# Shift and scale of layer 0: sums over input channels moved from TensorE to GpSimd and VectorE

## The chip, the core and the metric

One core of a Trainium2 chip runs the kernel. Five engines work side by side, each through its own queue in order: PE (TensorE; PEld are its weight loads), DVE (VectorE), ACT (ScalarE), POOL (GpSimd) and SP (SyncE, which here only issues DMAs). They meet at semaphores. The metric is the time of one execution in microseconds (us), the median of several runs.

## The reference

Two layers of a decoder trunk on x of 1024 positions by 1024 channels. Each layer begins with a normalisation of the rows of x that is modulated by the vector c; the modulation is what this document is about:

```python
c_act = jax.nn.silu(c)
for l in range(DEPTH):
    mod = c_act @ w_ada[l] + b_ada[l]
    shift, scale, gate = jnp.split(mod, 3, axis=-1)
    h = rmsnorm(x, g_pre[l]) * (1.0 + scale[:, None, :]) + shift[:, None, :]
    p = h @ w_in[l]
    ...
    y = jnp.concatenate([y_conv, y_attn], axis=-1) @ w_out[l]
    x = x + gate[:, None, :] * rmsnorm(y, g_post[l])
```

`w_ada` has 1024 input channels and 3072 columns. Between `p` and `y` lie a gated convolution and a sparse attention, which the change does not touch.

## The kernel before

All work on 1024 positions is cut into tiles of 128 rows (128 partitions). Matrix products that need full precision split each f32 operand into a high and a low part and make three passes (lines 87 to 89: high·high, high·low, low·high); the splitting of a weight is `load_w` (line 107 on ACT makes the high part, line 108 on POOL subtracts it).

Layer 0 begins in `first`. It needs four things from memory, all issued by SP in the order of the table `LOADS`: the eight row tiles of x (four in `xs` early, four late), the weights of shift and scale (`wa`), and the first columns of `w_in` (`wr`). The weights of shift and scale are laid out by output channel: chunk k of eight holds, for the 128 channels k, the 256 columns of shift and scale and all 1024 input channels. The input channels are cut into eight groups of 128, one channel of a group on each partition, so a chunk comes as two tiles of 128 x 1024, `ws[0]` with groups 0 to 3 and `ws[1]` with groups 4 to 7, and `ws[j // 4][:, j % 4]` is the 128 x 256 piece of group j. `cact` (128 x 8) holds silu(c) in the same layout.

`mod_cols(k, ...)` turns chunk k into 128 values of shift and 128 of scale. Eight matmuls of 32 output rows (line 171) multiply the pieces with `cact` and sum over the partitions and over groups j and j + 4; DVE copies the result out of PSUM (line 173); two matmuls against `sel` (line 176) add the four quarters and put the 256 sums on partitions. DVE adds the bias (line 179, `modc`) and makes the factor of the normalised row (line 180, `moda`).

The loop of `first` runs over k. It calls `mod_cols` for chunk k + 1 ahead of the work on chunk k, loads and splits `wr` on even k, and for chunk k and the first four row tiles transposes x (line 297, PE), applies `moda` and `modc` (line 299, ACT, into `hf`), splits into high and low (lines 301 and 302, DVE, into `hT`), and multiplies with the split `w_in` columns into four PSUM sums `cp` (12 matmuls per chunk). Only when all eight chunks are done come the last four row tiles (`columns(4, 8)`) and their products, and then the rest of the layer. The rows are normalised by a square sum on ACT (line 287), two small POOL instructions (lines 265 and 268, `rx`) and a multiplication on DVE (line 928).

The `wa` tiles use the buffers that `hT` takes over afterwards. The order of instructions in each engine's queue is not written by hand: a scheduler fixes it when the program is built, from the order of the code and its own estimate of times.

Of the kernel before, what the change touches and what calls it, by code (L numbers as in the profile page):

```python
# [19 lines left out]
OP = mybir.AluOpType  # L20
# [3 lines left out]
P = 128  # L24
# [27 lines left out]
def hybrid_kernel(ctx: ExitStack, tc: tile.TileContext, x, cT, w_ada, w_mod, bcol, bgate, g_pre, w_in, w_cp,  # L52
# [3 lines left out]
    V, S, G, T = nc.vector, nc.scalar, nc.gpsimd, nc.tensor  # L56
# [19 lines left out]
    def mm_ps(name="mm"):  # L76
        return ps.tile([P, 512], F32, name=name, tag="mm", bufs=2)
# [65 lines left out]
    cact = cst.tile([P, 8], F32, name="cact")  # L143
    V.scalar_tensor_tensor(cact, cth, 1.0, ct, op0=OP.add, op1=OP.mult)
    V.tensor_scalar(cact, cact, 0.5, None, op0=OP.mult)
    pick = cst.tile([P, 8], F32, name="pick")
    V.memset(pick, 0.0)
    V.memset(pick[:, 5:6], 1.0)
    for q in range(4):
        V.memset(pick[32 * q:32 * q + 1, q:q + 1], 1.0)  # L150
        V.memset(pick[32 * q:32 * q + 1, 4:5], 1.0)
    pick4, sel, ones = pick[:, 0:4], pick[:, 4:5], pick[:, 5:6]
    x1d = dr.tile([L, D], F32, name="x1d")
    gd = dr.tile([depth, 1024], F32, name="gd")
    ad = dr.tile([4, P, 1024], F32, name="ad")
# [7 lines left out]
        MOD[l] = (bc, gp, cst.tile([P, 2, 8], F32, name="modc", tag="modc"),  # L163
                  cst.tile([P, 8], F32, name="moda", tag="moda"))

    def mod_cols(k, ws, row):

        o = mm_ps("mod")
        for j in range(8):
            q = j % 4  # L170
            T.matmul(o[32 * q:32 * q + 32, :256], cact[:, j:j + 1].to_broadcast([P, 32]), ws[j // 4][:, j % 4],
                     start=j < 4, stop=j >= 4)
        V.tensor_copy(row, o[:, :256])
        t = mm_ps("modt")
        for j in range(2):
            T.matmul(t[:, j:j + 1], row[:, 128 * j:128 * j + 128], sel, start=True, stop=True)
        bc, gp, mc, a = MOD[0]
        ks = slice(k, k + 1)
        V.tensor_tensor(mc[:, :, ks], t[:, 0:2].rearrange("p (c h) -> p c h", c=2), bc[:, :, ks], op=OP.add)
        V.scalar_tensor_tensor(a[:, ks], mc[:, 1, ks], 1.0, gp[:, ks], op0=OP.add, op1=OP.mult)  # L180
# [198 lines left out]
    def first(xs, wa, wr):  # L379
# [14 lines left out]
        def mod(k):  # L394
            if k < 8:
                mod_cols(k, wa[k], row[:, k % 4])
                if k % 2 == 0:
                    c.w.append(load_cw(0, k // 2, wr[:, 456 * k:456 * k + 912]))
# [734 lines left out]
```

## Time and profile before

| | |
|---|---|
| median of 3 runs | 1255.23 us (1254.13 to 1255.27) |
| the profiled execution | 1254.51 us |
| its span, first to last instruction | 1252.8 us |
| busy share of the span | PE 95%, PEld 78%, DVE 73%, ACT 55%, POOL 50% |
| instructions | 23059 |

The span is the stretch from the first to the last instruction of the program; the execution's own time is 1.7 us longer. All stretches below are counted from the span's start. The profile gives busy time by engine, by stretch and by group of instructions; the idle time of an engine is put down to what ended it. A group's line names the line of the kernel, engine, operation, what is written and read, and the shape.

### The profile page before, as it was taken

What the parts mean: (1) busy time and instruction counts of PE and PEld (TensorE: products, weight loads), DVE (VectorE), ACT (ScalarE), POOL (GpSimd) and SP (SyncE); (2) the same over time, 40 slices, a digit from 0 to 9 for tenths busy, and PEclk for the clock granted to TensorE, in tenths of its full rate; (3) what the DMA queues carried; (4) which work ended last, traced back from release to release, by engine and by line L of the source; (5) the groups of instructions that cost most, each with busy time, mean ns of one, the idle gap of its engine ahead of it and who ended that gap; (6) DMA issues with size and microseconds to landing.
All of it is one profiled execution on the core that took longest, in us unless ns stands there. A gap on an engine that the chain in (4) does not pass through costs nothing. (4 is left out here: it accounts for less than half of the span.)

```text
span 1252.8 us, 23059 instructions
## 1 busy us (share of the span) xinstructions
PE 1188.3 (95%) x7832; PEld 974.9 (78%) x7832; DVE 915.3 (73%) x2239; ACT 688.1 (55%) x1580; POOL 628.0 (50%) x1222
## 2 busy tenths in 40 slices
PE   6999999898998999999999999989979899999998
PEld 3888888557886777789988888866768677777998
DVE  3667899999777667757686579989985866677214
ACT  3645768667626556522355466877682465564221
POOL 3441146447536457855585202554673465588222
PEclk9999999899999999999999999989989899999999
DMA  9411266771010000137751123767111100012215
GB/s 360 144 51 34 52 206 209 243 250 52 11 43 21 9 9 26 52 108 267 241 202 53 44 51 107 233 209 211 55 32 28 34 10 5 5 54 74 74 35 185
DMA packets 90854, 128.10 MB, mean 102 GB/s; under 512 B 41320, under 2 KB 68464, under 8 KB 90736
## 3 DMA queue, kind: packets, MB, share of 16 engines
q1 hardware_dynamic: 90736, 126.63, 31.6%
q8 instruction: 62, 1.02, 0.3%
q14 instruction: 56, 0.46, 0.1%
HBM read 114.01 MB, written 12.59 MB: 101 GB/s over the span
## 5 line engine op out<-in xcount | busy, mean ns | idle before, releaser
L528 DVE TENSOR_SCALAR_CACHE_REDUCE jv<-pl,cand 128x768 int16<-128x768 uint16 (+1 forms) x186 | 187.8, 1009 | 17.7 <-DVE jv L528 6.6
L525 ACT ACTIVATE ja<-pl,cand 128x896 int8<-128x896 uint16 (+1 forms) x186 | 153.8, 827 | 40.6 <-POOL cand L535 34.8
L803 ACT ACTIVATE p<-p,mx 128x128 f32<-128x128 f32 (+7 forms) x128 | 98.8, 772 | 55.1 <-DVE mx L800 53.1
L805 POOL TENSOR_SCALAR p<-p,ri 128x128 f32<-128x128 f32 (+7 forms) x128 | 99.8, 784 | 43.8 <-DVE ri L804 43.5
L108 POOL TENSOR_TENSOR wul<-raw,wuh 128x342 fp32r<-128x342 f32 (+1 forms) x48 | 48.6, 1022 | 132.1 <-ACT wuh L107 116.9
L89 PE MATMUL o<-woh,yl 128*128 128x256 f32 x384 | 108.7, 283 | 2.1 <-POOL yl L861 2.1
L87 PE MATMUL o<-woh,yh 128*128 128x256 f32 x384 | 109.4, 286 | 0.5 <-DVE yrr L903 0.5
L88 PE MATMUL o<-wol,yh 128*128 128x256 f32 x384 | 108.5, 283 | 0.0
L87 PE MATMUL g<-hT,wgh 128*128 128x512 f32 x256 | 103.3, 404 | 2.6 <-ACT ya L688 2.2
L89 PE MATMUL g<-hT,wgl 128*128 128x512 f32 x256 | 102.3, 399 | 0.0
L88 PE MATMUL g<-hT,wgh 128*128 128x512 f32 x256 | 101.6, 397 | 0.0
L87 PE MATMUL u<-hT,wuh 128*128 128x512 f32 x256 | 100.8, 394 | 0.0
L88 PE MATMUL u<-hT,wuh 128*128 128x512 f32 x256 | 100.0, 391 | 0.0
L89 PE MATMUL u<-hT,wul 128*128 128x512 f32 x256 | 99.9, 390 | 0.0
L817 PE MATMUL pt<-ident,p 128*128 128x128 f32 x576 | 94.6, 278 | 2.4 <-ACT pt L822 1.7
L790 POOL TENSOR_TENSOR p<-tb,score 128x256 f32<-128x256 f32 x96 | 71.2, 749 | 48.2 <-PE pt L817 46.1
L843 PE MATMUL av<-pt,v 128*64 128x256 f32 (+1 forms) x640 | 93.3, 368 | 0.0
L461 DVE SCALAR_TENSOR_TENSOR score<-relu,widx,score 128x384 f32<-128x384 f32 (+2 forms) x84 | 79.2, 976 | 18.4 <-ACT relu L453 17.5
L817 PEld LDWEIGHTS pt<-ident,p 128*128 128x128 f32 x576 | 67.4, 140 | 25.5 <-issue 10.9
L822 ACT ACTIVATE pt<-pt 128x512 f32<-128x512 f32 (+2 forms) x96 | 50.2, 523 | 64.4 <-PE pt L817 63.8
L453 ACT ACTIVATE relu<-ixs 128x512 f32<-128x512 f32 (+2 forms) x140 | 66.4, 522 | 34.5 <-PE ixs L447 34.1
L447 PE MATMUL ixs<-ix 128*128 128x512 f32 (+2 forms) x320 | 76.3, 356 | 0.4 <-DVE ix L436 0.4
(302 smaller groups left out, 3463.6 us busy)
## 6 DMA issues: line engine op xcount, KB each, us to landing
wt<-in_wl_dram SPq DMA_DIRECT2D x64, 512.0 KB, 5.1
wa<-in_w_mod_dram SPq DMA_DIRECT2D x32, 512.0 KB, 5.2
raw<-in_w_in_dram SPq DMA_DIRECT2D x64, 171.0 KB, 2.5
wa<-in_w_ada_dram SPq DMA_DIRECT2D x16, 512.0 KB, 9.8
raw<-in_w_out_dram SPq DMA_DIRECT2D x32, 171.0 KB, 2.4
raw<-in_w_in_dram SPq DMA_DIRECT2D x32, 170.0 KB, 2.6
ad<-A SPq DMA_DIRECT2D x8, 512.0 KB, 3.3
at<-ad SPq DMA_DIRECT2D x16, 256.0 KB, 6.5
```

Of the source, the lines that this page charges most:

```text
L87: T.matmul(o, ah, bh, start=first, stop=False)
L88: T.matmul(o, ah, bl, start=False, stop=False)
L89: return T.matmul(o, al, bh, start=False, stop=last)
L447: mark = T.matmul(o[:, :c1 - c0], s_[:, 128 * i:128 * i + 128], ix[:, kk, c0:c1], start=kk == 0, stop=kk == 1)
L461: V.scalar_tensor_tensor(acc, r[:, :w], wc, acc, op0=OP.mult, op1=OP.add)
L525: S.activation(ja[:, :wid(j)], src, AF.Sign, scale=-1.0, bias=col(cand, c), accum_out=col(ct_, c))
L528: V.tensor_scalar(jv[:, :wid(j)], src, col(cand, c), None, op0=OP.is_lt, op1=OP.add, accum_out=col(ct_, c))
L790: G.tensor_tensor(nb, tb, sc[:, OFF[i] + n0:OFF[i] + w], op=OP.add)
L803: mark[0] = S.activation(p[:, :w], p[:, :w], AF.Exp, scale=-1.0, bias=m[:, 2:3], accum_out=ri[:, 0:1])
L805: mark[1] = G.tensor_scalar(p[:, :w], p[:, :w], ri[:, 1:2], 1.0, op0=OP.mult, op1=OP.mult)
L817: T.transpose(t[:, 128 * j:128 * j + 128], p[:, 128 * (j0 + j):128 * (j0 + j) + 128], ident)
L843: T.matmul(o[64 * e:64 * e + 64, t0:256], lh, pts[e][j // 4][:, j % 4, t0:256], start=j == 0, stop=j == 2 * c + 1)
```

## The change

Only `mod_cols` changes. The sum over the eight groups of a partition's channels is taken out of the matmuls. Groups 0 to 2 are multiplied in place by `cact` on POOL and added into group 0 (three multiplications and two additions of 128 x 256). Group 3 is multiplied on DVE into a sum `acc`, groups 4 to 7 are multiplied and added on DVE, and at the end the POOL part is added. Two matmuls against a column of ones then sum over the partitions, where `sel` picked four rows before. PSUM holds no `mod` sum any more, and line 173's copy out of PSUM is gone. Lines behind the function move by 3 (299 becomes 302, 301 becomes 304, 302 becomes 305).

```diff
-    pick4, sel, ones = pick[:, 0:4], pick[:, 4:5], pick[:, 5:6]
+    pick4, ones = pick[:, 0:4], pick[:, 5:6]
...
-    def mod_cols(k, ws, row):
-
-        o = mm_ps("mod")
-        for j in range(8):
-            q = j % 4
-            T.matmul(o[32 * q:32 * q + 32, :256], cact[:, j:j + 1].to_broadcast([P, 32]), ws[j // 4][:, j % 4],
-                     start=j < 4, stop=j >= 4)
-        V.tensor_copy(row, o[:, :256])
+    def mod_cols(k, ws, acc):
+
+
+        for j in range(3):
+            G.tensor_scalar(ws[0][:, j], ws[0][:, j], cact[:, j:j + 1], 1.0, op0=OP.mult, op1=OP.mult)
+            if j:
+                G.tensor_tensor(ws[0][:, 0], ws[0][:, j], ws[0][:, 0], op=OP.add)
+        V.tensor_scalar(acc, ws[0][:, 3], cact[:, 3:4], None, op0=OP.mult)
+        for j in range(4, 8):
+            V.scalar_tensor_tensor(acc, ws[1][:, j - 4], cact[:, j:j + 1], acc, op0=OP.mult, op1=OP.add)
+        V.tensor_tensor(acc, acc, ws[0][:, 0], op=OP.add)
         t = mm_ps("modt")
-        for j in range(2):
-            T.matmul(t[:, j:j + 1], row[:, 128 * j:128 * j + 128], sel, start=True, stop=True)
+        for h in range(2):
+            T.matmul(t[:, h:h + 1], acc[:, 128 * h:128 * h + 128], ones, start=True, stop=True)
```

The scheduler places the new instructions among the old ones. On POOL, before, from the normalisation of the fourth row tile to that of the fifth (`wc1l` to `wc3` are low parts of `w_in`, three instructions each):

```order
L265 TENSOR_SCALAR rxv_278<-ssx_278 128x1
L268 TENSOR_TENSOR rx_280<-rxv_278,mhalf_71 128x1
L108 TENSOR_TENSOR wc1l_312<-wr_129,wc1h_311 128x304 x3
L108 TENSOR_TENSOR wc2l_402<-wr_129,wc2h_401 128x304 x3
L108 TENSOR_TENSOR wc3_491<-wr_129,wc3_491 128x304 x3
L265 TENSOR_SCALAR rxv_593<-ssx_591 128x1
```

On POOL, now, from the same place on (`wa_139`, `wa_143`, `wa_148`, `wa_152` are the first tiles of chunks 1, 2, 3 and 4):

```order
L268 TENSOR_SCALAR rxv_280<-ssx_278 128x1
L172 TENSOR_TENSOR wa_139<-wa_139 128x256
L271 TENSOR_TENSOR rx_282<-rxv_280,mhalf_71 128x1
L172 TENSOR_TENSOR wa_139<-wa_139 128x256
L170 TENSOR_SCALAR wa_143<-wa_143,cact_101 128x256 x3
L172 TENSOR_TENSOR wa_143<-wa_143 128x256 x2
L108 TENSOR_TENSOR wc1l_315<-wr_129,wc1h_314 128x304 x3
L170 TENSOR_SCALAR wa_148<-wa_148,cact_101 128x256 x3
L172 TENSOR_TENSOR wa_148<-wa_148 128x256
L170 TENSOR_SCALAR wa_152<-wa_152,cact_101 128x256 x3
```

The five instructions of each chunk stand between the splits of `w_in` and the normalisations that were alone there.

On DVE, before, around chunk 1 of the rows (`hT2` to `hT5`; `mrow` is the row that is copied out of PSUM):

```order
L173 COPY mrow_190<-mod_296 128x256
L301 CAST hT2_176<-hf_322 128x256
L302 TENSOR_TENSOR hT3_177<-hf_322,hT2_176 128x256
L301 CAST hT2_176<-hf_335 128x256
L179 TENSOR_TENSOR modc_122<-modt_306,bcol_118 128x2
L302 TENSOR_TENSOR hT3_177<-hf_335,hT2_176 128x256
L180 SCALAR_TENSOR_TENSOR moda_123<-modc_122,gpre_120 128x1
```

On DVE, now, around the same chunk (`mrow` is the sum `acc`):

```order
L173 TENSOR_SCALAR mrow_190<-wa_148,cact_101 128x256
L176 TENSOR_TENSOR mrow_190<-mrow_190,wa_143 128x256
L304 CAST hT2_176<-hf_325 128x256
L304 CAST hT2_176<-hf_338 128x256
L305 TENSOR_TENSOR hT3_177<-hf_325,hT2_176 128x256
L305 TENSOR_TENSOR hT3_177<-hf_338,hT2_176 128x256
L175 SCALAR_TENSOR_TENSOR mrow_190<-wa_149,cact_101,mrow_190 128x256 x2
L182 TENSOR_TENSOR modc_122<-modt_309,bcol_118 128x2
L175 SCALAR_TENSOR_TENSOR mrow_190<-wa_149,cact_101,mrow_190 128x256
L183 SCALAR_TENSOR_TENSOR moda_123<-modc_122,gpre_120 128x1
```

One copy has become six instructions a chunk; the last of them, line 176, reads what POOL wrote, and the multiplications and additions of the following chunks stand between the splits of `hT`. On PE the 64 matmuls of line 171 are gone and the rest keeps nearly its order. From the first score products of the attention on (line 447), all five queues hold the same instructions in the same order as before.

## Rows read from the trace of the kernel before

**Rows 1.** The page, first part: busy time, share of the span, instructions.

```profile
PE 1188.3 (95%) x7832; PEld 974.9 (78%) x7832; DVE 915.3 (73%) x2239; ACT 688.1 (55%) x1580; POOL 628.0 (50%) x1222
```

**Rows 2.** Stretches of 10 us: length, PE, PEld, DVE, ACT, POOL busy, clock, DMA share, GB/s.

```profile
10.00:20.00 10.00, 7.83 (x42) 4.00 (x38) 3.82 (x8) 3.90 (x8) 4.19 (x7) 1.00 1.03 420
20.00:30.00 10.00, 9.71 (x80) 6.74 (x73) 6.71 (x17) 4.79 (x11) 4.57 (x6) 1.00 1.03 417
30.00:40.00 10.00, 9.87 (x82) 7.45 (x81) 4.35 (x16) 3.56 (x8) 3.40 (x4) 1.00 1.03 409
40.00:50.00 10.00, 10.00 (x73) 7.74 (x73) 5.63 (x17) 7.24 (x15) 4.36 (x9) 1.00 0.18 42
```

**Rows 3.** Groups on PE, 9.9 to 49.4 us: count, busy us, mean ns, idle before.

```profile
L171 PE MATMUL mod<-wa,cact 128*32 128x256 f32 x128 | 11.1, 433 | 0.0
L176 PE MATMUL modt<-pick,mrow 128*128 128x1 f32 x32 | 4.7, 252 | 0.8 <-DVE mrow L173 0.8
```

**Rows 4.** Timeline, end of the first half: start, length, instruction.

```profile
49.31 0.15 DVE L180 SCALAR_TENSOR_TENSOR moda<-modc,gpre 128x1 f32<-128x1 f32 x1
49.56 1.02 ACT L299 ACTIVATE hf<-xt,modc,moda 128x256 f32<-128x256 f32 x2
...
52.32 0.47 PE L87 MATMUL cp<-wc,hT 128*128 128x456 f32 x1
...
54.08 0.99 PE L89 MATMUL cp<-wc,hT 128*128 128x456 f32 x4
```

**Rows 5.** The tile wa: its DMAs (issue times) and their time to landing.

```profile
L956 SPq DMA_DIRECT2D wa<-in_w_ada_dram x16: 328/328/515, 3.6 to 25.1; - x16
...
DMA to landing us min/median/max: 6.3/9.8/11.0
```

**Rows 6.** Groups on POOL by shape, whole program: count, busy us, mean ns, idle before.

```profile
L805 POOL TENSOR_SCALAR p<-p,ri 128x256 f32<-128x256 f32 x16 | 7.6, 477 | 5.6 <-DVE ri L804 5.4
L108 POOL TENSOR_TENSOR wvl<-raw,wvh 128x256 fp32r<-128x256 f32 x4 | 2.9, 738 | 7.9 <-ACT wvh L107 7.9
```

**Rows 7.** Groups on POOL, 9.9 to 49.4 us.

```profile
L268 POOL TENSOR_TENSOR rx<-rxv,mhalf 128x1 f32<-128x1 f32 x7 | 5.0, 715 | 0.6
L108 POOL TENSOR_TENSOR wc1l<-wr,wc1h 128x304 fp32r<-128x304 f32 x3 | 2.7, 925 | 5.9 <-ACT wc1h L107 5.9
...
L108 POOL TENSOR_TENSOR wc0l<-wr,wc0h 128x304 fp32r<-128x304 f32 x3 | 2.4, 825 | 2.1 <-ACT wc0h L107 2.1
```

**Rows 8.** Timeline: POOL and DVE alone (12.04, 26.94, 27.27) and together (23.19 on).

```profile
12.04 2.39 POOL L108 TENSOR_TENSOR wc0l<-wr,wc0h 128x304 fp32r<-128x304 f32 x3 [2.06 <-ACT wc0h L107]
...
23.19 2.69 POOL L108 TENSOR_TENSOR wc1l<-wr,wc1h 128x304 fp32r<-128x304 f32 x3 [5.94 <-ACT wc1h L107]
...
23.29 1.03 DVE L302 TENSOR_TENSOR hT<-hf,hT 128x256 fp32r<-128x256 f32 x1
...
24.29 0.88 DVE L301 CAST hT<-hf 128x256 fp32r<-128x256 f32 x1
...
26.94 0.29 DVE L301 CAST hT<-hf 128x256 fp32r<-128x256 f32 x1 [0.71 <-ACT hf L299]
...
27.27 0.43 DVE L302 TENSOR_TENSOR hT<-hf,hT 128x256 fp32r<-128x256 f32 x1
```

**Rows 9.** Timeline: two POOL instructions beside a run of DVE instructions.

```profile
62.91 4.36 POOL L108 TENSOR_TENSOR wul<-raw,wuh 128x342 fp32r<-128x342 f32 x2 [2.66 <-ACT wuh L107]
62.99 0.76 DVE L301 CAST hT<-hf 128x512 fp32r<-128x512 f32 x2
63.66 1.29 DVE L302 TENSOR_TENSOR hT<-hf,hT 128x512 fp32r<-128x512 f32 x2
64.86 0.43 DVE L301 CAST hT<-hf 128x512 fp32r<-128x512 f32 x1
```

**Rows 10.** Timeline: a POOL multiplication beside a DVE subtraction.

```profile
500.89 2.37 DVE L861 TENSOR_TENSOR yl<-yc,yh 128x1024 fp32r<-128x1024 f32 x1
502.16 2.09 POOL L805 TENSOR_SCALAR p<-p,ri 128x1024 f32<-128x1024 f32 x1
```

**Rows 11.** Stretches around an idle PE: length, PE busy, clock, DMA share, GB/s.

```profile
224.00:228.00 4.00, 1.97 (x22) 0.97 0.16 66
228.00:232.00 4.00, 0.18 (x4) 0.50 1.00 315
232.00:236.00 4.00, 4.00 (x36) 0.50 1.03 364
```

## Prediction

> **What bounds the kernel now.** I read the page first: PE is busy 95% of the span [rows 1], so time that PE waits more is time of the kernel, unless a later stage gives it back. Then the stretches of 10 us in which the change acts. From 20 us on PE is busy 9.7 to 10.0 of each 10 us, while POOL has 3.4 to 4.6 and DVE 4.4 to 6.7 [rows 2]. So in this stage PE sets the pace, and POOL stands idle more than half the time. The DMAs move 409 to 420 GB/s up to 40 us and 42 after that; the last `wa` is issued at 25.1 us and lands about 10 us later [rows 2, 5]. The weights are therefore no limit after 36 us, but the last `moda` is made at 49.31 us, and the last product of the first four row tiles is in the queue until about 54.7 [rows 4]. The stage before is 13 us behind its weights because PE has too much to do.
>
> On PE, line 171 has 128 records with 11.1 us of busy time, line 176 another 4.7 [rows 3]. That is the prize: some 11 us of the engine that bounds the stage. The question is whether the engines that take the work over can do it as fast as PE did.
>
> **What goes.** 64 matmuls leave PE: 11.1 us busy, 1.4 a chunk. Eight copies out of PSUM leave DVE. The 16 matmuls that remain are of the same shape as line 176 had, so 4.7 us stays. None of this is a gain by itself; it becomes one only if `moda` comes earlier than at 49.31.
>
> **What comes on POOL.** Five instructions a chunk. A multiplication of 128 x 256 by a column and by a constant is line 805's, 477 ns; an addition of 128 x 256 has its nearest row in line 108's subtraction of that size, 738 ns [rows 6]. So a chunk costs 3 x 0.477 + 2 x 0.738 = 2.91 us, eight chunks 23.3. POOL's old work between 10 us and the last addition: the four splits of `w_in`, 2.4 + 2.7 and two more of 2.6 each (0.85 an instruction or so) = 10.3, and two normalisations of 0.72 + 0.2 = 1.8 with one more small one [rows 7]. Together 35.4 us of POOL without a pause. POOL is free at about 10.0, when the first `wa` has landed, and finds all later chunks landed in time (the last at 36). So POOL's list ends at 45.4 at the earliest. Behind it come the last addition on DVE (0.43), the two matmuls, the bias and the factor: about 1.6 us, estimated from the same small steps of before. The last `moda` would be ready at 47.0 at best, against 49.46 before: **2.5 us earlier is the most that the change can bring**, and POOL, not PE, sets the pace then.
>
> **What comes on DVE, and what it does to POOL.** Six instructions a chunk, five of which read two tiles of SBUF. By busy time that fits: 48 x some 0.4 us = 19 us beside the 20 or so that DVE has from 10 to 50 us [rows 2, 8]. But the two engines do not run beside each other. First the rows: alone, three splits on POOL take 2.39 us, a cast on DVE 0.29 and a subtraction 0.43; when they meet at 23.19, the subtraction takes 1.03, the cast 0.88, and POOL's three take 2.69 [rows 8]. Each DVE instruction ends only after the POOL instruction that was under way. A POOL multiplication behaves alike: line 805 needs 2.09 us where a subtraction of DVE runs until 503.26, and it has only its last 1.0 us after that [rows 10].
>
> The price has two bounds. From 10 us to the last addition DVE issues about 54 instructions with two SBUF inputs (40 new, 14 subtractions of line 305), 22 casts and multiplications (8 new, 14 of line 304), and two normalisations of rows.
> - Strictly in turn: two DVE instructions cost POOL 2.69 - 2.39 = 0.30 us [rows 8], 0.15 each. 76 x 0.15 + 1 = 12 us. `moda` at 59, 10 us later than before.
> - In runs: where DVE instructions do not wait for each other, they keep POOL out. Between 62.99 and 65.29 five of them go past, and two splits that would take 1.9 us (0.825 for 304 columns [rows 7], scaled to 342) take 4.36 [rows 9]: POOL loses the whole run. Then an instruction costs its full pitch, about 0.33 (0.43 less the overlap of neighbours) or 0.20 for the short ones: 54 x 0.33 + 22 x 0.20 + 1.4 = 23.6. `moda` at 70.6, 21 us later.
>
> Below nothing the price can't go: no row shows POOL faster because DVE is busy. Which one? A chain of additions into one sum lets POOL in between its members; but the order now on DVE has casts, subtractions and multiplications of another chunk between these members, which depend on nothing before them, in about half of the places. I take the middle, 17.8 us: `moda` at 47.0 + 17.8 = 64.8, **15.3 us later** than 49.46.
>
> **What is late next.** Before, PE had 5.4 us of products left after the last `moda` (49.31 to 54.7), since it was behind [rows 4]. Now it has nothing but the last chunk: the activation and the splits of `hT`, then 12 products at 0.2 us. About 4.2 us, so 1.2 us come back. The normalisations of the last four row tiles stand on POOL beside and behind the last chunk's additions; four of them need 4 x 0.9 us and DVE's multiplications, which ends beside the last products, so I cost them at nothing; if they don't fit, up to 2 us are added. The other 10 us of PE's savings are lost as waiting. After that stage the queues hold the same work in the same order and PE is busy all the time, so nothing gives the delay back.
>
> **Sum.** Against the profiled execution's own 1254.51 us (span 1252.8 and 1.7 outside it; the median of the runs, 1255.23, is 0.7 higher): 1254.5 + 15.3 - 1.2 = 1268.6. By the two bounds: 1254.5 + 10 - 1.2 = 1263 and 1254.5 + 21 - 1.2 = 1274.
>
> [...]
>
> **The rivals.**
> - [...] 5%.
> - Strictly in turn, cheap end: only 0.10 to 0.15 us each, `moda` 5 to 10 us later: 1259 to 1263. For it: the additions do form a chain. Against it: the order on DVE. 17%.
> - Full exclusion: POOL loses each DVE instruction's whole time, and the clock comes on top: 1274 and more. [...] 12%. [...]
> - A wash: POOL's list and PE's old pace come out alike (price 2 to 5 us), 1254 to 1258. 4%.
>
> **How the numbers follow.** The forecast has what remains, 62%, with 1263 to 1273 as its own range. The strict turn and the full exclusion lie on its two sides. The range of 8 in 10 takes in most of both: 1260 to 1275. A measurement of this kernel can tell about 0.2% (2.5 us) from no change: faster by more, 4%; within it, 5%; slower, 91%.
>
> **What would show it.** In the profile of the changed kernel: POOL busy nearly all of each 10 us from 10 to 60 us, against 3.4 to 4.6 now; lines 170 and 172 with means well over 0.48 and 0.74 us, since waiting for DVE counts as busy; line 175 on DVE well over 0.43; PE busy 5 to 7 of 10 us in the same stretch, waiting for DVE's `mrow` at line 179 and for `hT`; the last `moda` at 60 to 69 us; and from there on every stage shifted by one amount. Wrong would be: POOL with pauses before 40 us, lines 170 and 172 at their clean price, or a last `moda` before 55 us. The part I trust least is the price per DVE instruction on POOL, which rests on two meetings of the engines.

## The result, and the profile after

| | before | after |
|---|---|---|
| median | 1254.97 us (1254.13 to 1255.27) | 1269.06 us (1268.91 to 1269.5) |
| the profiled execution | 1254.51 us | 1268.95 us |
| its span | 1252.8 us | 1267.2 us |
| instructions | 23059 | 22873 |

The ratio after to before is 1.0114, with a 95% interval of 1.0096 to 1.0131: the changed kernel is 14.1 us slower. The forecast was 1268.6. The total is right to half a microsecond, but two of its terms are not, as will be seen.

The page of after, its first part, answers to [rows 1]. PE has the same busy time with 128 instructions less; POOL has 28 us more and DVE 27 us more.

```profile
PE 1188.3 (94%) x7704; PEld 976.8 (77%) x7704; DVE 942.5 (74%) x2279; ACT 686.7 (54%) x1580; POOL 656.4 (52%) x1262
```

That PE's busy time did not fall, though it lost 11 us of work, is the first hint that PE ran part of this stage slowly. The stretches of 10 us of after, with the columns of [rows 2]:

```profile
10.00:20.00 10.00, 3.86 (x14) 2.99 (x13) 7.71 (x14) 3.90 (x8) 9.66 (x15) 1.00 1.03 421
20.00:30.00 10.00, 6.10 (x17) 3.47 (x15) 9.48 (x16) 2.15 (x6) 9.84 (x14) 1.00 1.03 419
30.00:40.00 10.00, 9.50 (x35) 7.95 (x35) 9.91 (x20) 2.53 (x7) 8.42 (x12) 1.00 1.03 410
40.00:50.00 10.00, 7.89 (x34) 6.16 (x34) 9.84 (x21) 3.19 (x7) 8.61 (x12) 0.83 0.18 45
50.00:60.00 10.00, 7.68 (x28) 5.80 (x28) 9.42 (x25) 4.09 (x9) 6.90 (x10) 0.72 0.00 0
60.00:70.00 10.00, 9.41 (x52) 8.00 (x52) 8.38 (x16) 6.89 (x18) 6.29 (x9) 0.94 0.21 54
```

The DMAs are as they were (410 to 421 GB/s up to 40 us). DVE (third busy time) is full from 20 to 60 us, POOL (fifth) up to 30 and less after that. PE has 14 to 35 matmul instructions in a stretch where it had 42 to 82, yet is busy 7.7 to 9.5 from 30 us on.

The groups of after on POOL and on DVE, 10 to 64 us (count, busy us, mean ns, idle before), with what [rows 6 to 8] gave for the same shapes: 0.477 for the multiplication, 0.738 for the addition, 0.825 for a split, and on DVE 0.43 for the subtraction and 0.29 for the cast.

```profile
L170 POOL TENSOR_SCALAR wa<-wa,cact 128x256 f32<-128x256 f32 x24 | 16.5, 701 | 0.0
L172 POOL TENSOR_TENSOR wa<-wa 128x256 f32<-128x256 f32 x16 | 13.1, 826 | 0.3
L108 POOL TENSOR_TENSOR wc2l<-wr,wc2h 128x304 fp32r<-128x304 f32 x3 | 2.9, 972 | 1.6 <-ACT wc2h L107 1.6
L108 POOL TENSOR_TENSOR wc<-wr,wc 128x304 fp32r<-128x304 f32 x3 | 2.7, 911 | 1.4 <-ACT wc L107 1.4
L268 POOL TENSOR_SCALAR rxv<-ssx 128x1 f32<-128x1 f32 x6 | 2.6, 438 | 3.4 <-ACT ja L290 3.0
```

```profile
L175 DVE SCALAR_TENSOR_TENSOR mrow<-wa,cact,mrow 128x256 f32<-128x256 f32 x32 | 21.6, 678 | 0.3
L305 DVE TENSOR_TENSOR hT<-hf,hT 128x256 fp32r<-128x256 f32 x14 | 8.8, 637 | 0.0
L304 DVE CAST hT<-hf 128x256 fp32r<-128x256 f32 x14 | 7.1, 514 | 0.8 <-ACT hf L302 0.7
L176 DVE TENSOR_TENSOR mrow<-mrow,wa 128x256 f32<-128x256 f32 x8 | 4.9, 618 | 0.1
```

Both engines are stretched, not POOL alone. And the last group tells which of the two is later: line 176 adds what POOL wrote, and DVE stood idle only 0.1 us before its eight additions. For the sums DVE never waited for POOL; POOL's part of a chunk lay ready 0.4 to 7.4 us before DVE came to it, for the first and the last chunk only 0.4.

What that does to the rest is in the waits of after, 10 to 64 us (who waits, for what, us in total, times, longest). ACT, which turns transposed rows into `hf`, stands 24 us:

```profile
ACT hf L302 <- DVE moda L183: 24.0, 5, 6.9
PE xt L300 <- DVE xt L931: 13.0, 3, 9.7
PE modt L179 <- DVE mrow L176: 5.9, 5, 3.5
```

The end of the first half of after answers to [rows 4]. First DVE: the last addition of POOL's part at 59.71, the last `moda` at 64.90, which was at 49.31.

```profile
59.71 0.41 DVE L176 TENSOR_TENSOR mrow<-mrow,wa 128x256 f32<-128x256 f32 x1
...
64.70 0.16 DVE L182 TENSOR_TENSOR modc<-modt,bcol 128x2 f32<-128x2 f32 x1 [0.27 <-PE modt L179]
64.90 0.16 DVE L183 SCALAR_TENSOR_TENSOR moda<-modc,gpre 128x1 f32<-128x1 f32 x1
```

Then PE in the same time:

```profile
57.24 0.73 PE L87 MATMUL cp<-wc2h,hT 128*128 128x456 f32 x1
57.77 0.58 PE L88 MATMUL cp<-wc2l,hT 128*128 128x456 f32 x1
...
63.54 0.37 PE L88 MATMUL cp<-wc,hT 128*128 128x456 f32 x1
...
64.17 0.50 PE L179 MATMUL modt<-pick,mrow 128*128 128x1 f32 x4
...
68.50 0.99 PE L89 MATMUL cp<-wc,hT 128*128 128x456 f32 x4
```

The row of sums is complete at 60.1, but its sum over partitions (line 179) runs at 64.17: it stands behind two chunks of products in PE's queue, and the first of these take 0.58 us each instead of 0.37. The granted clock reads 0.50 there; it fell at 54.5 us, after PE had been busy 0.69 of 2 us from 52 to 54 (length, PE busy, clock, DMA share, GB/s):

```profile
52.00:54.00 2.00, 0.69 (x2) 1.00 0.00 0
57.00:59.00 2.00, 2.00 (x8) 0.50 0.00 0
```

From there on the shift is constant. The first score product stood at 92.10 us before (first fence) and stands at 106.51 after (second fence), 14.4 later, which is also the difference of the spans.

```profile
92.10 0.97 PE L447 MATMUL ixs<-ix 128*128 128x384 f32 x4
```

```profile
106.51 0.97 PE L450 MATMUL ixs<-ix 128*128 128x384 f32 x4
```

This place serves as the yardstick below: a kernel's shift there differs by at most 2.1 us from the difference of its time, and it does not contain the jitter of the other 1150 us.

### The profile page after: what moved, and what is told of

Read it like the earlier page. It is cut to its first block, busy times and chain, and to the rows that moved or that the text cites. A ratio compares the mean times of both kernels' runs of the same rounds, so it can differ in the third digit from the quotient of the medians.

```text
span 1267.2 us, 22873 instructions
## 1 busy us (share of the span) xinstructions
PE 1188.3 (94%) x7704; PEld 976.8 (77%) x7704; DVE 942.5 (74%) x2279; ACT 686.7 (54%) x1580; POOL 656.4 (52%) x1262
## 5 line engine op out<-in xcount | busy, mean ns | idle before, releaser
L806 ACT ACTIVATE p<-p,mx 128x128 f32<-128x128 f32 (+7 forms) x128 | 98.7, 772 | 54.5 <-DVE mx L803 52.6
L793 POOL TENSOR_TENSOR p<-tb,score 128x256 f32<-128x256 f32 x96 | 71.1, 748 | 48.4 <-PE pt L820 46.6
L825 ACT ACTIVATE pt<-pt 128x512 f32<-128x512 f32 (+2 forms) x96 | 50.3, 523 | 65.1 <-PE pt L820 64.5
```

The costliest lines, as they stand in the source:

```text
L793: G.tensor_tensor(nb, tb, sc[:, OFF[i] + n0:OFF[i] + w], op=OP.add)
L806: mark[0] = S.activation(p[:, :w], p[:, :w], AF.Exp, scale=-1.0, bias=m[:, 2:3], accum_out=ri[:, 0:1])
```

## The experiments

### Each engine alone

Two kernels take one engine's part of the sums away. The first, GpSimd alone:

```diff
-        V.tensor_scalar(acc, ws[0][:, 3], cact[:, 3:4], None, op0=OP.mult)
-        for j in range(4, 8):
-            V.scalar_tensor_tensor(acc, ws[1][:, j - 4], cact[:, j:j + 1], acc, op0=OP.mult, op1=OP.add)
-        V.tensor_tensor(acc, acc, ws[0][:, 0], op=OP.add)
+        acc = ws[0][:, 0]
```

> Layer 0's shift and scale from channel groups 0 to 2 alone: POOL does its five instructions a chunk as in the changed kernel, the six of VectorE and groups 3 to 7 are left out. Theory A (the two engines shut each other out at SBUF): POOL's instructions cost little more than alone, line 170 at 0.48 to 0.55 us against 0.70 in the changed kernel, line 172 at 0.74 to 0.79 against 0.83; last moda at 47 to 52 us, time 1253 to 1258. Theory B (POOL's list of some 35 us is itself the bound): last moda where it was, 62 to 66, time 1266 to 1270. Theory C (VectorE's queue is too long by itself): last moda before 49, time 1250 to 1254.

The second, VectorE alone, drops the three multiplications and two additions on GpSimd and the last addition on VectorE.

> The counterpart: VectorE does groups 3 to 7 as in the changed kernel (one multiplication, four multiply-adds a chunk), POOL's five instructions, the last addition and groups 0 to 2 are left out. Theory A: line 175 at 0.43 to 0.50 us against 0.68 in the changed kernel, last moda at 45 to 49 us, time 1250 to 1254. Theory B: the same, since POOL has no part in it. Theory C: VectorE still sets the end, last moda after 58, time over 1262.

Measured, in one run each: 1259.44 us with GpSimd alone, first score product 5.1 us later than before; 1256.49 us with VectorE alone, 2.7 us later. Together, in the changed kernel, it is 14.4: 6.6 more than the sum of the two. Neither list alone explains the loss; the rest comes only when both engines work. The times lie 1.4 and 2.5 us above what theory A expected (first value beside B's 1266 and C's 1254, second beside C's 1262), so neither hits the number, and A is the nearest in both. A's other numbers were too low as well: the last `moda` came at 54.5 us (A: 47 to 52) and at 52.1 (45 to 49), line 170 took 0.58 us, and the multiply-adds of VectorE alone 0.53 in the mean; only line 172, at 0.78, was in its range. With VectorE alone the 26 multiply-adds beside which no POOL instruction ran took 0.48 us, the other six 0.76.

POOL's groups with GpSimd alone, 10 to 64 us, show the stretch shrink from 701 and 826 ns:

```profile
L170 POOL TENSOR_SCALAR wa<-wa,cact 128x256 f32<-128x256 f32 x24 | 13.5, 577 | 0.1
L172 POOL TENSOR_TENSOR wa<-wa 128x256 f32<-128x256 f32 x16 | 12.3, 778 | 0.3
```

POOL's last addition there begins at 48.23 and takes 0.73 us, so its list ends at 49.0: 3.6 us after the 45.4 of a clean list, through the splits of `hT` and the rows' normalisation that DVE still does.

### The second SBUF input of VectorE's sums

The same work on both engines, but VectorE's running sum lies in PSUM, so that a multiply-add reads one SBUF tile instead of two.

```diff
-        V.tensor_scalar(acc, ws[0][:, 3], cact[:, 3:4], None, op0=OP.mult)
+        p = mm_ps("mod")[:, :256]
+        V.tensor_scalar(p, ws[0][:, 3], cact[:, 3:4], None, op0=OP.mult)
         for j in range(4, 8):
-            V.scalar_tensor_tensor(acc, ws[1][:, j - 4], cact[:, j:j + 1], acc, op0=OP.mult, op1=OP.add)
-        V.tensor_tensor(acc, acc, ws[0][:, 0], op=OP.add)
+            V.scalar_tensor_tensor(p, ws[1][:, j - 4], cact[:, j:j + 1], p, op0=OP.mult, op1=OP.add)
+        V.tensor_tensor(acc, p, ws[0][:, 0], op=OP.add)
```

> All of the changed kernel's work on the same engines in the same number of instructions, but VectorE's running sum lies in PSUM, so that each of its five multiply-adds and additions a chunk reads only one tile of SBUF and none reads two. Theory A: line 175 at 0.40 to 0.50 us, line 170 at 0.48 to 0.58; what is left of the collision is that with the splits of hT; last moda at 50 to 56 us, time 1255 to 1262. Theories B and C: no engine has less to do, time as the changed kernel, 1267 to 1271.

Measured: 1260.92 us (ratio to before 1.0047, 1.003 to 1.0064), first score product 5.1 us later. That is the shift of GpSimd alone (97.17 and 97.16): at this place VectorE's whole share, with its sum in PSUM, costs nothing beside GpSimd's. 9.3 of the 14.4 us are gone (8.1 by the medians) through an operand's place, with every instruction kept. The order is not kept: POOL's queue is the same through its last addition, but the scheduler laid out VectorE's in another order from about 21 us on, and PE's with it. In the other experiments, too, queues come in other orders. So the shift alone can't part the operand from the order; the durations below can. The time and the last `moda` (55.5) are where A put them, line 170 lies just above (0.595 against 0.58). The groups of this kernel, 10 to 64 us, on POOL and on DVE:

```profile
L170 POOL TENSOR_SCALAR wa<-wa,cact 128x256 f32<-128x256 f32 x24 | 13.9, 595 | 0.0
L172 POOL TENSOR_TENSOR wa<-wa 128x256 f32<-128x256 f32 x16 | 12.5, 787 | 0.3
```

```profile
L176 DVE SCALAR_TENSOR_TENSOR mod<-wa,cact,mod 128x256 f32<-128x256 f32 x32 | 15.5, 484 | 0.5
L306 DVE TENSOR_TENSOR hT<-hf,hT 128x256 fp32r<-128x256 f32 x16 | 10.2, 650 | 0.0
L305 DVE CAST hT<-hf 128x256 fp32r<-128x256 f32 x16 | 6.7, 422 | 0.9 <-ACT hf L303 0.9
L177 DVE TENSOR_TENSOR mrow<-mod,wa 128x256 f32<-128x256 f32 x8 | 3.3, 419 | 0.7 <-POOL wa L172 0.4
```

The multiply-adds fall from 678 to 484 ns, which over 32 of them is 6.2 of the 9.3 us, and POOL's multiplications from 701 to 595; the subtractions of `hT`, which still read two SBUF tiles, stay at 650.

So beside a busy POOL the multiply-adds with one SBUF input are not held, 484 ns against the 0.48 us of VectorE alone with no POOL instruction beside, and the subtractions with two are, 650 ns against 430 alone. Two inputs are not the only case: the casts, which read one tile of SBUF, are held too (422 ns against 290 alone), and no run shows why.

### All groups on VectorE

Nothing on GpSimd, one multiplication and seven multiply-adds on VectorE, first with the sum in SBUF, then in PSUM.

```diff
-        for j in range(3):
...
-        V.tensor_scalar(acc, ws[0][:, 3], cact[:, 3:4], None, op0=OP.mult)
-        for j in range(4, 8):
...
+        V.tensor_scalar(acc, ws[0][:, 0], cact[:, 0:1], None, op0=OP.mult)
+        for j in range(1, 8):
+            V.scalar_tensor_tensor(acc, ws[j // 4][:, j % 4], cact[:, j:j + 1], acc, op0=OP.mult, op1=OP.add)
```

> POOL's part moved to VectorE: one multiplication and seven multiply-adds a chunk, 64 instructions in place of 48, none on POOL. Theory A: 64 x some 0.42 us without a partner to wait for, with the 16 us of hT and row work between: last moda at 50 to 56 us, time 1255 to 1262. Theory B: POOL's list is gone, last moda before 49, time 1250 to 1254. Theory C: VectorE has more than in the changed kernel, time over 1270.

> All eight groups on VectorE and none on GpSimd, as in the run that took 1262.5, but with the running sum in PSUM instead of SBUF, so that each of its instructions reads one SBUF tile. Theory A (two SBUF inputs are what VectorE and GpSimd exclude each other by): a multiply-add takes 0.42 to 0.46 us instead of 0.555, GpSimd's splits return to 0.83 to 0.90, and the time is 1256 to 1259. Rival C (the number of instructions in VectorE's queue is the bound, whatever they read): 1261 to 1264.

Measured: 1262.48 us (1.0059, 1.004 to 1.0078) with the sum in SBUF, 8.0 us later at the first score product; 1263.99 us (1.0073, 1.006 to 1.0086) in PSUM, 11.0 later. The first lies just over A's upper end, and its last `moda` (57.5) too. The second falls in C's range: as A said, three of the four splits on POOL are back at 0.82 to 0.85, but the multiply-adds take 0.49 us, more than A's 0.46, and it is not faster. With the sum in SBUF DVE is busy 10.0 of each 10 us from 20 to 50 us, so there its own queue is the limit; with the sum in PSUM it is busy 9.7 to 8.0 from 20 to 60 us, and that the number of its instructions decides fits but is not shown. Why the PSUM version is even 3 us later is not settled. The scheduler laid out a different order, in which PE waits 7.7 us for `hf` against 1.2 (and 3.9 for the sums against 7.3), and in which multiply-adds that follow each other always do so 0.51 to 0.53 us apart (21 pairs), while with the sum in SBUF 17 of 25 pairs are 0.40 apart. The groups on DVE, 10 to 62 us, SBUF first, then PSUM:

```profile
L171 DVE SCALAR_TENSOR_TENSOR mrow<-wa,cact,mrow 128x256 f32<-128x256 f32 x56 | 29.5, 555 | 0.3
```

```profile
L173 DVE SCALAR_TENSOR_TENSOR mod<-wa,cact,mod 128x256 f32<-128x256 f32 x48 | 23.4, 487 | 0.7
```

This pair also shows the hold without any difference in the work of POOL, which has only its splits and normalisations here. With the sum in SBUF a multiply-add takes 0.478 us when no POOL instruction is under way (33 of them) and 0.665 beside one (23). With the sum in PSUM it takes 0.485 in either case (35 and 21).

### Which of the two is the later one

By the first runs the changed kernel's loss lies between the engines, not in one list. Which queue ends it? Two kernels shift one group of channels, to two on GpSimd or to four:

```diff
-        for j in range(3):
+        for j in range(2):
...
-        V.tensor_scalar(acc, ws[0][:, 3], cact[:, 3:4], None, op0=OP.mult)
-        for j in range(4, 8):
-            V.scalar_tensor_tensor(acc, ws[1][:, j - 4], cact[:, j:j + 1], acc, op0=OP.mult, op1=OP.add)
+        V.tensor_scalar(acc, ws[0][:, 2], cact[:, 2:3], None, op0=OP.mult)
+        for j in range(3, 8):
+            V.scalar_tensor_tensor(acc, ws[j // 4][:, j % 4], cact[:, j:j + 1], acc, op0=OP.mult, op1=OP.add)
```

> The changed kernel with two groups of channels on GpSimd instead of three, and six on VectorE instead of five. First score product of the changed kernel: 14.4 us later than before; with no group on GpSimd and all on VectorE it was 8.0 later. Theory E (VectorE's queue is the later one, and its time is stretched by what GpSimd holds it up): about 2 us come back per group taken from GpSimd, first score product 11 to 13 us later than before, time 1265.5 to 1268. Theory B (GpSimd's list, with what VectorE adds to it, is the later one; it loses 3 of 8 steps that take 0.70 and 0.83 us each, 12.2 us in all): 2 to 7 us later, 1257 to 1262.

> The changed kernel with four groups on GpSimd and four on VectorE. Theory E: GpSimd gets 16 more instructions of 0.70 and 0.83 us, 12.2 us, has only 6 us of pauses to put them in, and becomes the later one: first score product 20 to 27 us later than before, time 1275 to 1282. Theory C (the number of instructions in VectorE's queue sets the end in the changed kernel, whatever GpSimd does): VectorE loses 8 of 48, first score product 9 to 12 us later, time 1263 to 1267.

Measured: 1266.53 us (1.0092, 1.0078 to 1.0106), 11.8 us later, with two groups; 1277.13 us (1.0177, 1.0162 to 1.0193), 24.2 later, with four. Both fall where theory E put them. Taking 16 instructions from GpSimd and giving eight to VectorE, whose queue is the later one, makes the kernel 2.5 us faster by the medians and 2.6 at the first score product; the intervals of the two ratios overlap a little (1.0078 to 1.0106 and 1.0096 to 1.0131). The rows agree: the multiply-adds take 630 ns instead of 678 and the casts 355 instead of 514, so that VectorE's 87 instructions of 256 columns in `mod_cols` and in the splits of `hT` (10 to 64 us) take 46.9 us in all, against 46.1 for the 76 of the changed kernel, and POOL's part of a chunk lies ready 2.3 to 10.5 us before VectorE's last addition. What VectorE's queue loses is set by how often GpSimd holds it. With a fourth group it turns around, and the group of DVE's last additions with four groups (10 to 64 us) shows it, since DVE now waits for POOL:

```profile
L176 DVE TENSOR_TENSOR mrow<-mrow,wa 128x256 f32<-128x256 f32 x8 | 6.2, 781 | 7.9 <-POOL wa L172 7.9
```

Of the 24.2 us, 17.9 stand at the last `moda` (67.16 against 49.31). The rest comes behind it: the last products of the first half begin 11.5 us after it there, 5.4 before.

### The clock, and PE's queue

In the changed kernel PE has gaps, a granted clock of 0.50 in two stretches, and a wait of 4 us of the last sums in its queue. Theory D was that PE's relief itself costs time. So PE gets its eight matmuls per chunk back, with a result that nobody reads, once in the changed kernel and once in the one with VectorE alone:

```diff
     def mod_cols(k, ws, acc):
+        o = mm_ps("mod")
+        for j in range(8):
+            q = j % 4
+            T.matmul(o[32 * q:32 * q + 32, :256], cact[:, j:j + 1].to_broadcast([P, 32]), ws[1][:, j % 4],
+                     start=j < 4, stop=j >= 4)
```

> The changed kernel, and beside it PE also does the eight matmuls of before in each chunk (the pieces of the second tile twice, the sums are used by nobody), so that PE has before's work in this stage again. Theory D (in the changed kernel PE, relieved, stands idle in gaps, its granted clock falls to 0.50, and the last sums over partitions then stand behind products at half speed): the granted clock stays at 1.00 from 40 to 62 us, products there are 0.2 us apart instead of 0.38, the last scale factor comes 1.5 to 3 us earlier than at 64.9, and the time is 1266 to 1268, so more work on PE makes it faster. Rival (PE's relief was a small gain that the wait for GpSimd and VectorE only covers): 1269 to 1273.

> VectorE's five groups alone, GpSimd's three left out (so shift and scale are wrong: three of eight groups of input channels are missing), with the eight matmuls of before kept on PE for nobody. Without the kept matmuls this kernel took 1256.5, its last sums stood in PE's queue from 48.45 to 51.3 us behind products at half clock. Theory D: clock 1.00 through 30 to 50 us, last scale factor at 49 to 50.5 instead of 52.1, time 1253.5 to 1255.5, in spite of 11 us more work on PE. Rival (PE's relief is a gain and VectorE's queue is what is late): 1257.5 to 1262.

Measured: 1271.11 us (1.0128, 1.0114 to 1.0142) and 1256.69 us (1.0014, 1.0003 to 1.0025). The first is in the rival's range, the second between the two. The medians are 2.1 and 0.2 us above those without the matmuls, with intervals that overlap in the first pair and a single run in the second; the first score product stands at 106.48 against 106.51 without the matmuls, and at 94.41 against 94.80. So 11 us of work more or less on PE, together with the clock that comes with it, moves this stage by 0.4 us at most; the two were not tried apart. As a price, D fell.

As a mechanism it was there in part. With VectorE alone and no matmuls kept, the last row of sums is complete at 48.45 us, and its sums over partitions stand in the queue until 51.32 behind products, the first of which (44.0 to 47.4) took 0.58 us each instead of 0.37, with a granted clock of 0.83 in the mean of 40 to 50 us:

```profile
44.04 0.75 PE L87 MATMUL cp<-wc2h,hT 128*128 128x456 f32 x1
44.58 0.58 PE L88 MATMUL cp<-wc2l,hT 128*128 128x456 f32 x1
...
51.32 0.50 PE L174 MATMUL modt<-pick,mrow 128*128 128x1 f32 x4
```

With the matmuls kept they run at 49.12, and the last `moda` is at 50.32 instead of 52.05; in the changed kernel with matmuls kept it is at 62.12 instead of 64.90, though the clock did fall once more there, against D (0.83 from 50 to 60 us). But most of this lies ahead of PE's queue: the last row of sums was complete earlier, at 46.6 instead of 48.45 and at 58.6 instead of 60.1. From there to `moda` it is 3.7 us against 3.6 in the one pair and 3.5 against 4.8 in the other. And the gain is lost behind `moda`, where a second chain is as late: the square sums of the last four row tiles wait in ACT's queue behind `hf`, POOL's `rx` waits for them, and the multiplication of the row on DVE for `rx`. In the changed kernel with matmuls kept POOL waits 2.15 us for a square sum until 61.44 (first fence), and DVE's last normalised row ends at 65.41 + 0.75 = 66.2 (second fence); without the matmuls it ended at 65.15 + 1.27 = 66.4 (third fence, the changed kernel). In the pair with VectorE alone it ends at 53.8 against 54.1. These ends moved by 0.2 and 0.3 us, as little as the first score product did.

```profile
61.44 0.19 POOL L273 TENSOR_SCALAR rxv<-ssx 128x1 f32<-128x1 f32 x1 [2.15 <-ACT ja L295]
```

```profile
65.41 0.75 DVE L936 TENSOR_SCALAR x<-x,rx 128x1024 f32<-128x1024 f32 x1 [0.24 <-POOL rx L276]
```

```profile
65.15 1.27 DVE L931 TENSOR_SCALAR x<-x,rx 128x1024 f32<-128x1024 f32 x1
```

So two chains end together: one through PE's queue and `moda`, one through ACT's queue and the normalisation. Both start at the late sums.

### A version that relieves PE and nothing else

Some chunks go to VectorE, with the sum in PSUM, the others stay on PE as before, and GpSimd gets nothing. First chunks 1, 3 and 5, then only 3 and 5:

```diff
+        dve = k in (1, 3, 5)
+        if dve:
+            p = mm_ps("mod")[:, :256]
+            V.tensor_scalar(p, ws[0][:, 0], cact[:, 0:1], None, op0=OP.mult)
+            for j in range(1, 8):
+                V.scalar_tensor_tensor(row if j == 7 else p, ws[j // 4][:, j % 4], cact[:, j:j + 1], p, op0=OP.mult, op1=OP.add)
+        else:
...
-            T.matmul(t[:, j:j + 1], row[:, 128 * j:128 * j + 128], sel, start=True, stop=True)
+            T.matmul(t[:, j:j + 1], row[:, 128 * j:128 * j + 128], ones if dve else sel, start=True, stop=True)
```

> Chunks 1, 3 and 5 by VectorE with the sum in PSUM, the other five chunks by PE as before, nothing on GpSimd. PE loses three times 1.4 us and keeps enough to have no gaps. Theory D (relief of PE is worth its full size as long as PE is not left idle): clock 1.00 from 20 us on, end of the first half's products 3 to 4 us earlier than 54.7, time 1250.5 to 1252. Theory A with its price on GpSimd's splits and VectorE's own queue deciding: 1254 to 1258.

> Chunks 3 and 5 by VectorE with the sum in PSUM, the other six by PE as before, nothing on GpSimd. With chunks 1, 3 and 5 the granted clock rose to 1.00 only at 25.4 us instead of 19.6, which at half speed costs PE 2.9 us, as much as three chunks of eight matmuls take off it (1.0 us each at full clock). Theory D (only that late clock ate the relief): here chunk 1 is back on PE, the clock is at 1.00 from about 20 us again, first score product 1.5 to 2.2 us earlier than before, time 1252.5 to 1253.5. Rival (another chain, the rows' normalisation and the splits of hT on VectorE, is as late as PE anyway): within 0.5 us of before, 1254 to 1255.5.

Measured: 1253.92 us (0.9991, 0.9981 to 1.0), first score product 0.6 us later than before, and 1255.69 us (1.001, 1.0001 to 1.0019), 0.4 us earlier. Both ratios lie within 0.1% of before, and neither version beats the kernel before; the first is outside D's range and 0.1 us below A's, the second 0.2 above the rival's. With chunks 1, 3 and 5 PE was without a gap over 0.25 us from 20 to 55 us, but slow for longer: the sixteen records of a chunk's sums took 1.84 us at 23.74 (first fence), where before they took 1.07 at 21.50 (second fence).

```profile
23.74 1.84 PE L178 MATMUL mod<-wa,cact 128*32 128x256 f32 x16
```

```profile
21.50 1.07 PE L171 MATMUL mod<-wa,cact 128*32 128x256 f32 x16
```

With chunk 1 back on PE the last `moda` came at 47.6, 1.7 us earlier than before, as theory D wanted; still only 0.4 us of it reached the first score product, which is the rival's number. That the relief is lost to the rows' normalisation, whose last `rx` begins at 50.2 there against 49.2, fits but was not tried by itself.

## Why the prediction came out right

The mechanism was right: the two engines hold each other up, the last `moda` comes some 15 us later for it, and nothing behind gives that back. That the number was right to half a microsecond is luck, as the terms show.

**POOL's clean list** was put at 45.4 us. With GpSimd alone it ended at 49.0, with DVE's old work beside it. Right, as a lower end. Its prices hold: with GpSimd alone the six multiplications and six additions beside which no DVE instruction ran took 0.479 and 0.727 us. Line 805 before, by shape (medians, 0.371 us for 128 elements to 1.12 for 1024), takes 0.84 ns an element and 0.26 us besides.

**The price on POOL** was put at 17.8 us, between 12 and 23.6. This is the step that was mis-sized. From the groups above: 24 x (0.701 - 0.477) = 5.4, 16 x (0.826 - 0.738) = 1.4, 12 x (0.950 - 0.825) = 1.5 (the mean of the twelve splits), 8.3 us in all. That is under the cheap bound of 12, "strictly in turn". The two meetings of [rows 8, 9] had given 0.15 to 0.33 us per DVE instruction; the 76 cost 0.11 each. The bound rests on a misreading of [rows 8]: POOL's three splits met three DVE instructions, not two. The third is the row below (before); it begins while POOL works, until 25.88. So 0.30 us were 0.10 each, and 76 x 0.10 + 1 = 8.6 is what the row would have given, beside the 8.3 measured.

```profile
25.21 0.95 DVE L302 TENSOR_TENSOR hT<-hf,hT 128x256 fp32r<-128x256 f32 x1
```

What took the place of the other 9.5 us:
- POOL's pauses, 1.6 + 1.4 + 3.0 = 6.0 us, each ended by ACT. The fence below has ACT of after ahead of the first and the last: what POOL wanted stood in ACT's queue behind `hf`, which waited for `moda`, and so for DVE's sums (ahead of the second one it waited for DVE's splits of `hT`). The list had been counted without a pause. 45.4 + 8.3 + 6.0 = 59.7, and POOL's last addition ended at 59.3.

```profile
35.62 1.02 ACT L302 ACTIVATE hf<-xt,modc,moda 128x256 f32<-128x256 f32 x2 [5.15 <-DVE moda L183]
36.54 1.14 ACT L107 ACTIVATE wc2h<-wr 128x304 fp32r<-128x304 f32 x3
...
55.83 1.02 ACT L302 ACTIVATE hf<-xt,modc,moda 128x256 f32<-128x256 f32 x2 [6.87 <-DVE moda L183]
56.74 1.05 ACT L290 ACTIVATE ja<-x 128x1024 int8<-128x1024 f32 x1
```

- The way from the last addition to `moda`, put at 1.6 us, is 59.3 to 65.1, 5.8 us, of which 4 are the wait in PE's queue. "The same small steps of before" had an idle PE queue in mind, and it was not idle.

So 17.8 + 1.6 = 19.4 was forecast, and 8.3 + 6.0 + 5.8 = 20.1 came, by other ways. The last `moda`, ready at 65.06 against 64.8, is agreement in the sum, not in its terms: 9.5 us too much in one stood in for 10.2 us that were in none.

**Whose queue.** The argument named POOL as the engine that sets the pace and asked only what DVE costs it. The other direction is the larger one: DVE's multiply-adds lost 32 x (0.678 - 0.482) = 6.3 us, the subtractions 14 x (0.637 - 0.43) = 2.9, the casts 14 x (0.514 - 0.29) = 3.1, the last additions 8 x (0.618 - 0.42) = 1.6: 13.9 us against POOL's 8.3. (0.482 is the median of that instruction with VectorE alone, in the row below: min, median, max; 0.42 is line 177 with the sum in PSUM.) DVE was the later one, as the 0.1 us of idle time before line 176 and the runs with two and four groups show; for the last chunk only by 0.4 us, since POOL had stood still for 3.0 just before. "By busy time that fits" (19 us beside 20) was wrong as soon as each instruction took 0.2 us longer.

```profile
L171 DVE SCALAR_TENSOR_TENSOR mrow<-wa,cact,mrow x17: 472/482/1064, 31.2 to 48.0; 128x256 f32<-128x256 f32 x17
```

**What is late next.** 4.2 us after the last `moda` were forecast, and the last products of the first half begin at 69.1, 4.2 after it. The normalisations were costed at nothing, and in the sum they are; but the last normalised row ended at 66.4, 1.4 us after the last `moda`, and so a gain in `moda` alone is lost, as with the kept matmuls.

**The rest.** "Nothing gives the delay back" holds: 14.4 us at 106.5 and 14.4 in the span.

**The rivals.** "A wash" (4%) is out, and so is a faster kernel (4%): POOL lost 8.3 us and DVE 13.9 beside each other. "Strictly in turn" was right on POOL's price and wrong on the time, for the pauses and PE's queue that it left out. The clock that "full exclusion" puts on top did fall (0.50 in two stretches of after between 44 and 61 us), but that hardly got through: giving PE its work back, with the granted clock at 1.00, 0.83 and 1.00 in the stretches from 40, 50 and 60 us instead of 0.83, 0.72 and 0.94, moved the first score product by 0.0 us; with VectorE alone, at 1.00 from 30 to 50 us instead of 0.83, by 0.4.

**The signs.** Right: lines 170 and 172 stretched, line 175 well over 0.43, the last `moda`, the constant shift. Wrong: PE busy 5 to 7 of 10 us, since a slow PE is busy longer (7.7 to 9.5 from 30 us on); POOL busy nearly all the time, which ends at 35.5 us with the first pause. A pause before 40 us was named as a sign of being wrong, and rightly: it pointed at the pauses that the list left out.

## What to carry to other kernels

Before sums go from PE to VectorE and GpSimd together, count the SBUF inputs of VectorE's instructions: one running sum in PSUM instead of SBUF was worth 9.3 of 14.4 us here with the same instructions on the same engines, if in another order. Price the hold in both directions, since the engine that loses less may be the one that was thought the bound (POOL's 8.3 us against DVE's 13.9 here). Count every instruction that runs beside a stretched one before a price per instruction is taken from it: three instead of two would have given the right price here. And a saving on the busiest engine is worth only what the next chain leaves of it: 11 us of PE's work, given back, moved the first score product by 0.4 us at most once other queues were the later ones.

## What the runs showed of the hardware that was not expected

- A multiply-add that continues the sum of the one before it begins 0.52 us after it, wherever the sum lies, more than the 0.40 or so at which other instructions follow. With VectorE alone (sum in SBUF) ten of the twelve pairs beside which POOL stood idle are 0.51 to 0.52 apart and two 0.40; by their place these two begin another chunk's sum. In the PSUM version of all groups all twelve such pairs are 0.52 to 0.53 apart (two rows below). There 21 pairs stand so, which at 0.12 us each would be 2.5 us of DVE's time.

```profile
50.25 0.48 DVE L173 SCALAR_TENSOR_TENSOR mod<-wa,cact,mod 128x256 f32<-128x256 f32 x1
50.77 0.48 DVE L173 SCALAR_TENSOR_TENSOR mrow<-wa,cact,mod 128x256 f32<-128x256 f32 x1
```

- In the changed kernel products read 0.58 us up to 37 us and 0.37 after, though the stretch view prints a granted clock of 1.00 for all of 10 to 40 us. The duration is what PE did; the 1.00 that is printed ahead of 37 us is not to be relied on.
